# Weight units of a hybrid decoder layer placed at byte offsets 0, 32, 64 or 96 in their SBUF tiles

## The chip, the cores and the metric

The kernel runs on one core of one Trainium2 chip, in one launch. The metric is device time in microseconds (us) from the first to the last moment of the execution; lower is better. Each kernel is run several times and the median is compared. A profile of one execution shows what every engine of the core did: PE (TensorE: matmuls, with PEld for the loading of weights into the array), DVE (VectorE), ACT (ScalarE), POOL (GpSimd), SP (which issues most DMAs).

## The reference

One decoder layer on 512 tokens of width 1024, all in float32. Cut to what matters:

```python
h = rmsnorm(x)
q, k, v, xr, gr, g_attn, g_rnn = split(h @ w_in)        # w_in: 1024 x 7168
A = diff_attention(q, k, v)                              # 8 heads, causal, two softmaxes, shared bias
R = gelu(gr) * rg_lru(causal_conv4(xr))
x = x + (sigmoid(g_attn) * (A @ w_proj_attn) + sigmoid(g_rnn) * (R @ w_proj_rnn)) @ w_out
x = x + square(relu(rmsnorm(x) @ w_up)) @ w_down         # 1024 -> 4096 -> 1024
```

## The kernel before

Every large product runs as three matmuls of type float32r on TensorE (`mm3`, lines 125 to 127): each operand is split into a high part and the remainder, and hi*hi, hi*lo and lo*hi are added in PSUM. A matmul has a *stationary* operand of 128x128, which is loaded into the array beforehand by a weight load, and a *moving* operand of 256 or 512 columns, which is streamed through. The profile writes out<-in with the names of both. While one matmul streams its moving operand, the weight load of the next one reads its stationary operand, so two reads from SBUF run side by side nearly all the time.

Weights come in *units* of 128x1024 numbers (four k tiles of 256 columns). SP loads a raw unit (`wraw`, later `raw`), ACT rounds it into `whi`, DVE writes the remainder into `wlo`. There are four buffers of each kind in pool `wp`, and one more pair in pool `fin` for the MLP, which takes every fifth unit there (`own`). Class `Weights` keeps one queue of units each for attention (`wa`) and for the recurrent branch (`wb`); `cols` puts requests into it, `cast` splits a unit, `get` hands it out. The MLP has its own list of units (`ops`, `cast_hi`, `cast_lo`).

The stages, with the sides on which the weight units stand:

- gates: `cols_proj` with weights stationary and `hT` (the normed input, transposed) moving, 512 columns. The same form serves the recurrent projections, then the attention projection (`aT` moving), the recurrent projection (`R`), the output projection (`mT`), and the MLP's up projection (`h2T` moving).
- q, k, v: `tok_proj` has tokens of `hT` stationary and the weight units `whi`, `wlo` *moving*, 256 columns. Four head pairs j = 0 to 3, filled in between the steps of attention.
- MLP down (line 1093): seven products of a Strassen-like scheme, weights stationary, the squared activations `us` moving, 256 columns. The up projection fills `us` in four chunks d, and after each chunk two halves m of the down projection follow.

The order on each engine is the order in which the program is written (helper `InOrder`; most ACT, DVE and POOL rows therefore carry line 66). The placement of tiles in SBUF is that of the pools. As built, every `whi` and `wlo` buffer in `wp` starts at a byte address that leaves 64 when divided by 128 (25920, 30016, 34112, 38208 and 42304, 46400, 50496, 54592), and the pair in `fin` at one that leaves 0. `hT`, `mT` and one of three `us` buffers (units of chunks n with n % 3 = 0) leave 64, `h2T`, `R`, `hu` and the other two `us` buffers leave 0, and `aT` leaves 96. Offsets within these tiles are multiples of 512 bytes, so every operand keeps the remainder of its tile.

Of the kernel before, what the change touches and what calls it, by code (L numbers as in the profile page):

```python
# [12 lines left out]
F32R = mybir.dt.float32r  # L13
# [6 lines left out]
P = 128  # L20
# [3 lines left out]
KT = DM // P  # L24
# [13 lines left out]
def tile_block(ctx: ExitStack, tc: tile.TileContext, x, w_in, w_rga, w_rgx, w_pa, w_pr, w_o,  # L38
# [5 lines left out]
    wp = ctx.enter_context(tc.tile_pool(name="wp", bufs=3))  # L44
# [13 lines left out]
    class InOrder:  # L58
        def __init__(self, engine):
            self.engine = engine  # L60
# [15 lines left out]
    def psum(tag):  # L76
        return pp.tile([P, 512], F32, tag=tag, name=tag, bufs=nb[tag])

    slots = [4]

    class Weights:
        def __init__(self, ahead, raws):
            self.reqs, self.raw, self.units = [], [], []
            self.pos, self.done, self.ahead, self.raws = 0, 0, ahead, raws

        def cols(self, w, c0, k0=0, n=KT):
            for k0 in range(k0, k0 + n, 4):
                self.reqs.append((w[k0 // 4, c0 // 256], 4))
            return self

        def fetch(self):
# [3 lines left out]
                nc.sync.dma_start(raw, src.rearrange("p (k c) -> p k c", k=a))  # L95
                self.raw.append(raw)

        def cast(self, pool=None):
            assert pool or slots[0] > 0
            slots[0] -= 0 if pool else 1  # L100
            self.fetch()
            n = len(self.units)
            raw, a = self.raw[n], self.reqs[n][1]
            hi, lo = ((pool or wp).tile([P, a, 1024 // a], F32R, tag=t, name=t, bufs=2 if pool else 4) for t in ("whi", "wlo"))
            A.copy(hi, raw)
            V.tensor_tensor(out=lo, in0=raw, in1=hi.bitcast(F32), op=ALU.subtract)
            self.raw[n] = None
            self.units.append((hi, lo))
            self.fetch()
# [14 lines left out]
    def mm3(o, l, r, first, last):  # L124
        T.matmul(o, l[0], r[0], start=first, stop=False)  # L125
        T.matmul(o, l[0], r[1], start=False, stop=False)  # L126
        T.matmul(o, l[1], r[0], start=False, stop=last)  # L127

    def split(hi, lo, src, scale=None):
        if scale is None:  # L130
            A.copy(hi, src)
            V.tensor_tensor(out=lo, in0=src, in1=hi.bitcast(F32), op=ALU.subtract)
        else:
            A.activation(hi, src, AF.Copy, scale=scale)
            V.scalar_tensor_tensor(out=lo, in0=src, scalar=scale, in1=hi.bitcast(F32), op0=ALU.mult, op1=ALU.subtract)
# [67 lines left out]
    def rstd_of(dst, ss, n, width):  # L203
        t = sm.tile([P, width], F32, tag="ms", name="ms")
        V.tensor_scalar(out=t, in0=ss, scalar1=1.0 / n, scalar2=EPS, op0=ALU.mult, op1=ALU.add)
        G.tensor_tensor(out=dst, in0=t, in1=mhalf[:, :width], op=ALU.pow)
# [22 lines left out]
    OQ, OK_, OV, OX, OG, OGA, OGR = (j * DM for j in range(7))  # L229
    wa = Weights(2, 2)  # L230
    wa.cols(w_in, OGA + 512)
    for j in range(4):
        for o in (OQ, OK_, OV):
            wa.cols(w_in, o + 256 * j)
    wa.cols(w_in, OGA + 768)
    for j in range(4):
        wa.cols(w_in, OGR + 256 * j)
    for j in range(4):
        wa.cols(w_pa, 256 * j)
    wb = Weights(1, 1)  # L240
    for j in range(4):
        wb.cols(w_in, OX + 256 * j).cols(w_in, OG + 256 * j)
    for j in range(4):
        wb.cols(w_pr, 256 * j)
    for j in range(4):
        wb.cols(w_o, 256 * j)
    R, aT, mT = [None] * KT, [None] * NH, [None] * KT
    tgr, tga = [None] * KT, [None] * KT
    es_act = ExitStack()
# [15 lines left out]
    with tc.tile_pool(name="p1", bufs=1) as p1:  # L265
        on = p1.tile([P, P], F32, name="on")
        G.memset(on, 1.0)
        zero = p1.tile([P, 256], F32R, name="zero")
        V.memset(zero.bitcast(F32), 0.0)
        pw = psum("acc")  # L270
        for n in range(16):
            T.matmul(pw[:, :256], zero[:, :P], zero, start=True, stop=True)
        ssq = p1.tile([P, S], F32, name="ssq")
        xT = p1.tile([P, KT, S], F32, name="xT")
        hu = [p1.tile([P, KT, S], F32R, name=f"hu{z}", tag=f"hu{z}") for z in range(2)]
        raws = [[(wp if u else p1).tile([P, 4, 256], F32, name="wraw", tag="wraw", bufs=2) for u in range(2)] for z in range(2)]
        pieces = ((0, 1), (1, 2), (2, 4), (4, 6), (6, 8))
        for k0, k1 in pieces:
            nc.sync.dma_start(xT[:, k0:k1, :], x[k0 * P:k1 * P, :].rearrange("(k p) s -> p k s", p=P))
            if k0 == 0:  # L280
                nc.sync.dma_start(smt, smalls)
            for z in range(2):
                c0 = 256 * (k0 % 4)
                nc.sync.dma_start(raws[z][k0 // 4][:, k0 % 4:(k1 - 1) % 4 + 1, :],
                                  w_in[k0 // 4, OGA // 256 + z][:, c0:c0 + 256 * (k1 - k0)].rearrange("p (k c) -> p k c", c=256))
        wa.fetch()
        ws = [[[wp.tile([P, 4, 256], F32R, tag=t, name=t, bufs=4) for t in ("whi", "wlo")] for u in range(2)] for z in range(2)]
        ps = [[psum("at"), psum("at")] for z in range(2)]
        for k0, k1 in pieces:
            u, kk = k0 // 4, slice(k0 % 4, (k1 - 1) % 4 + 1)  # L290
            for k in range(k0, k1):
                split(hu[0][:, k, :], hu[1][:, k, :], xT[:, k, :], smt[:, C_G1 + k:C_G1 + k + 1])
                if k == k0:
                    for z in range(2):
                        split(ws[z][u][0][:, kk, :], ws[z][u][1][:, kk, :], raws[z][u][:, kk, :])
            for k in range(k0, k1):
                sq = ssq if k == 0 else p1.tile([P, S], F32, tag="sq", name="sq", bufs=2)
                A.activation(sq, xT[:, k, :], AF.Square)
                if k:
                    V.tensor_tensor(out=ssq, in0=ssq, in1=sq, op=ALU.add)  # L300

        def two(k):
            for z in range(2):
                for c in range(2):
                    w = ws[z][k // 4]
                    cs = slice(c * P, (c + 1) * P)
                    mm3(ps[z][c], (w[0][:, k % 4, cs], w[1][:, k % 4, cs]), (hu[0][:, k, :], hu[1][:, k, :]), k == 0, k == KT - 1)

        for k in range(6):
            two(k)  # L310
        slots[0] = 2
        wa.cast()
        pr = psum("at")
        for t in range(NT):
            T.matmul(pr[:, t:t + 1], ssq[:, t * P:(t + 1) * P], ones, start=True, stop=True)
        rs = sm.tile([P, NT], F32, tag="rs4", name="rs4")
        rstd_of(rs, pr[:, :NT], DM, NT)
        dg = p1.tile([P, S], F32, name="dg", tag="sq", bufs=2)
        for t in range(NT):
            A.activation(dg[:, t * P:(t + 1) * P], ident, AF.Copy, scale=rs[:, t:t + 1])  # L320
        two(6)
        wa.cast()
        rb = p1.tile([P, S], F32, name="rb")
        gu = cols_proj(wa, lambda k: (hu[0][:, k, :], hu[1][:, k, :]), lambda ps: gate_out(tga, 2, ps, rb))
        pb = psum("acc")
        T.matmul(pb, on, dg, start=True, stop=True)
        V.tensor_copy(rb, pb)
        two(7)
        slots[0] += 2
        for k in range(KT + 1):  # L330
            if k < KT:
                V.tensor_tensor(out=xT[:, k, :], in0=xT[:, k, :], in1=rb, op=ALU.mult)
            if k > 0:
                split(hT[0][:, k - 1, :], hT[1][:, k - 1, :], xT[:, k - 1, :], smt[:, C_G1 + k - 1:C_G1 + k])
                next(gu)
        wa.pump()
        for z in range(2):
            gate_out(tga, z, ps[z], rb)
# [482 lines left out]
    fin = ctx.enter_context(tc.tile_pool(name="fin", bufs=1, reuse_waits="tile"))  # L821
# [79 lines left out]
    added, cast = set(), set()  # L901
# [12 lines left out]
    def cast_hi():  # L914
        n = len(units)
        plus(n)
        slots[0] -= 1
        kind, a, p = ops[n]
        src = raw[kind, a, p if kind == "up" else uses[p][0]]
        own = n % 5 == 4  # L920
        hi, lo = ((fin if own else wp).tile([P, 4, 256], F32R, tag=t, name=t, bufs=1 if own else 4) for t in ("whi", "wlo"))
        A.copy(hi, src)
        units.append((hi, lo))
        half.append((hi, lo, src, ops[n]))
# [19 lines left out]
    def ahead():  # L944
        if half:
            cast_lo()
        if can_cast():
            cast_hi()
# [105 lines left out]
    for n, (kind, a, p, pairs) in enumerate(steps):  # L1054
        o = kind, a, p
# [11 lines left out]
        hi, lo = units[number[o]]  # L1067
# [19 lines left out]
        k = seen.get(o, 0)  # L1087
# [53 lines left out]
```

## Time and profile before

| | |
|---|---|
| time, median of 3 runs | 880.63 us (880.16 to 881.45) |
| the profiled execution | 880.92 us, its span 879.2 us |
| PE busy | 871.2 us, 5232 matmuls |
| PEld busy | 762.6 us |
| DVE / ACT / POOL busy | 602.2 / 429.0 / 64.4 us |
| DMA | 99.28 MB, mean 113 GB/s |

Times in the profile count from the start of the span. Busy time of PE is the union of its matmuls, which overlap: a matmul's duration in the table of groups is longer than the distance from its start to the next start. What PE costs is therefore read from that distance (here called the *cadence*), in a stretch of known matmuls.

### The profile page before, as it was taken

What the parts mean: (1) busy time and instruction counts of PE and PEld (TensorE: products, weight loads), DVE (VectorE), ACT (ScalarE), POOL (GpSimd) and SP (SyncE); (2) the same over time, 40 slices, a digit from 0 to 9 for tenths busy, and PEclk for the clock granted to TensorE, in tenths of its full rate; (3) what the DMA queues carried; (4) which work ended last, traced back from release to release, by engine and by line L of the source; (5) the groups of instructions that cost most, each with busy time, mean ns of one, the idle gap of its engine ahead of it and who ended that gap; (6) DMA issues with size and microseconds to landing.
All of it is one profiled execution on the core that took longest, in us unless ns stands there. A gap on an engine that the chain in (4) does not pass through costs nothing.

```text
span 879.2 us, 13193 instructions
## 1 busy us (share of the span) xinstructions
PE 871.2 (99%) x5232; PEld 762.6 (87%) x5232; DVE 602.2 (68%) x1040; ACT 429.0 (49%) x683; POOL 64.4 (7%) x72
## 2 busy tenths in 40 slices
PE   9999999999999999999999999999999999999997
PEld 7799999999888887888878888889988998899897
DVE  6765688887866346877876656767746775667586
ACT  7444355554555336577643235556335444544441
POOL 0030222113000000000000000000000000000000
PEclk9999999999999999999999999999999999999999
DMA  5347222131321342322213633223642364256353
GB/s 200 135 142 222 93 73 77 52 94 62 98 70 39 113 137 95 110 85 88 80 55 125 223 125 114 102 86 82 170 166 72 110 173 134 64 137 194 78 146 95
DMA packets 34238, 99.28 MB, mean 113 GB/s; under 512 B 3952, under 2 KB 8760, under 8 KB 34176
## 3 DMA queue, kind: packets, MB, share of 16 engines
q1 hardware_dynamic: 30976, 87.93, 30.3%
q0 software_dynamic: 3200, 10.50, 6.3%
q8 instruction: 41, 0.67, 0.3%
q14 instruction: 21, 0.17, 0.1%
HBM read 87.89 MB, written 4.76 MB: 105 GB/s over the span
## 4 chain that ended last, share of the span: by engine, by line
PE 88%; ACT 4%; DMA 3%; DVE 3%; issue 1%; SPq 0%; POOL 0%; ACTq 0%; DVEq 0%; POOLq 0%
PE acc L125 21%; PE acc L126 21%; PE acc L127 20%; PE acc L1093 17%; PE at L507 3%; DMA wraw<-in_w_in_dram 2%; ACT whi L66 1%; DVE wlo L66 1%; PE at L541 1%; PE at L126 1%; PE at L127 1%; PE at L125 1%; PE at L459 1%; PE at L572 1%; DMA xT<-in_x_dram 1%
## 5 line engine op out<-in xcount | busy, mean ns | idle before, releaser
L1093 PE MATMUL acc<-us,whi 128*128 128x256 f32 x896 | 158.9, 281 | 0.5 <-DVE x L66 0.5
L66 DVE TENSOR_TENSOR wlo<-wraw,whi 128x1024 fp32r<-128x1024 f32 (+2 forms) x86 | 96.9, 1148 | 67.9 <-ACT whi L66 67.6
L66 ACT CAST whi<-raw 128x1024 fp32r<-128x1024 f32 x88 | 90.5, 1048 | 104.2 <-DVE raw L66 39.4
L1093 PEld LDWEIGHTS acc<-us,whi 128*128 128x128 f32 x896 | 137.7, 189 | 1.2 <-DVE x L66 0.7
L1093 PE MATMUL acc<-us,wlo 128*128 128x256 f32 x448 | 125.4, 280 | 0.0
L66 DVE TENSOR_TENSOR wlo<-raw,whi 128x1024 fp32r<-128x1024 f32 x88 | 106.8, 1220 | 17.1 <-ACT whi L66 17.0
L125 PE MATMUL acc<-whi,hT 128*128 128x256 f32 x384 | 111.4, 290 | 0.0
L127 PE MATMUL acc<-whi,hT 128*128 128x256 f32 x384 | 108.9, 284 | 0.0
L126 PE MATMUL acc<-wlo,hT 128*128 128x256 f32 x384 | 108.9, 284 | 0.0
L66 ACT CAST whi<-wraw 128x1024 fp32r<-128x1024 f32 (+2 forms) x86 | 82.5, 982 | 50.0 <-DMA wraw<-in_w_in_dram 33.6
L126 PE MATMUL acc<-h2T,whi 128*128 128x512 f32 x256 | 100.5, 392 | 0.0
L125 PE MATMUL acc<-h2T,whi 128*128 128x512 f32 x256 | 100.1, 391 | 0.0
L127 PE MATMUL acc<-h2T,wlo 128*128 128x512 f32 x256 | 100.0, 390 | 0.0
L1093 PEld LDWEIGHTS acc<-us,wlo 128*128 128x128 f32 x448 | 84.2, 188 | 0.0
L125 PE MATMUL acc<-hT,whi 128*128 128x512 f32 x208 | 82.2, 395 | 0.0
L127 PE MATMUL acc<-hT,wlo 128*128 128x512 f32 x208 | 81.5, 392 | 0.0
L126 PE MATMUL acc<-hT,whi 128*128 128x512 f32 x208 | 81.5, 392 | 0.0
L125 PEld LDWEIGHTS acc<-whi,hT 128*128 128x128 f32 x384 | 73.2, 191 | 4.3 <-issue 3.0
L127 PEld LDWEIGHTS acc<-whi,hT 128*128 128x128 f32 x384 | 73.2, 191 | 0.8 <-issue 0.4
L126 PEld LDWEIGHTS acc<-wlo,hT 128*128 128x128 f32 x384 | 73.3, 191 | 0.7 <-issue 0.5
L66 ACT ACTIVATE pe<-pe,nm 128x128 f32<-128x128 f32 (+3 forms) x64 | 35.5, 556 | 65.4 <-DVE nm L66 65.4
L66 DVE TENSOR_TENSOR x<-acc,x 128x512 f32<-128x512 f32 x48 | 33.0, 688 | 40.9 <-PE acc L1093 31.5
(194 smaller groups left out, 1609.9 us busy)
## 6 DMA issues: line engine op xcount, KB each, us to landing
wraw<-in_w_in_dram SPq DMA_DIRECT2D x52, 512.0 KB, 3.5
raw<-in_w_up_dram SPq DMA_DIRECT2D x32, 512.0 KB, 4.4
raw<-in_w_dn_dram SPq DMA_DIRECT2D x32, 512.0 KB, 3.4
raw<-raw POOLq DMA_DIRECT2D x16, 512.0 KB, 4.5
wraw<-in_w_pa_dram SPq DMA_DIRECT2D x8, 512.0 KB, 4.3
wraw<-in_w_pr_dram SPq DMA_DIRECT2D x8, 512.0 KB, 3.4
wraw<-in_w_o_dram SPq DMA_DIRECT2D x8, 512.0 KB, 4.4
trep<-tdram SPq DMA_DIRECT2D x8, 320.0 KB, 4.9
```

Source lines behind the costliest of these rows:

```text
L66: ins = f(*a, **k)
L125: T.matmul(o, l[0], r[0], start=first, stop=False)
L126: T.matmul(o, l[0], r[1], start=False, stop=False)
L127: T.matmul(o, l[1], r[0], start=False, stop=last)
L459: T.transpose(out=ps[:, t * P:(t + 1) * P], in_=qn[t // 2][:, c0:c0 + P], identity=ident)
L507: T.matmul(lg[c][:, :N], qT[r, x0, i * P:(i + 1) * P], kT[r, y0, :N], start=a == 0, stop=a == 2)
L541: T.transpose(out=tp[:, b * P:(b + 1) * P], in_=st[s][:, b * P:(b + 1) * P], identity=ident)
L572: T.matmul(ps[:, t:t + 1], sq[:, t * P:(t + 1) * P], ones, start=True, stop=True)
L1093: T.matmul(b[:, 256 * u:256 * u + 256], l[:, i, P * u:P * u + P], act[:, r, f, i % 2], start=p in ("M1", "M2", "M5") and k == z == u == e ...
```

## The change

A helper `weight_pair` makes every pair of `whi` and `wlo`. The tiles get 32 more numbers (128 bytes) per partition, and the unit lies 8 * shift numbers, that is 32 * shift bytes, behind the tile's start. `shift` is 0 to 3: the head pair j for q, k and v, the output group j in the other projections (0 for the two gate groups OGA + 512 and OGA + 768 and for the first two groups), a // 2 % 4 for a unit of the MLP's up projection, and (2 * chunk + half) % 4 for the down projection. Two arguments that were never used (`k0`, `n` of `cols`, and `pool` of `cast`) go.

```diff
+    def weight_pair(a, shift, own=None):
+        ts = [(own or wp).tile([P, 1024 + 32], F32R, tag=t, name=t, bufs=1 if own else 4) for t in ("whi", "wlo")]
+        return [t[:, 8 * shift:8 * shift + 1024].rearrange("p (k c) -> p k c", k=a) for t in ts]
...
-            hi, lo = ((pool or wp).tile([P, a, 1024 // a], F32R, tag=t, name=t, bufs=2 if pool else 4) for t in ("whi", "wlo"))
+            hi, lo = weight_pair(a, self.shift[n])
...
     for j in range(4):
         for o in (OQ, OK_, OV):
-            wa.cols(w_in, o + 256 * j)
+            wa.cols(w_in, o + 256 * j, j)
     wa.cols(w_in, OGA + 768)
     for j in range(4):
-        wa.cols(w_in, OGR + 256 * j)
+        wa.cols(w_in, OGR + 256 * j, j)
...
-        ws = [[[wp.tile([P, 4, 256], F32R, tag=t, name=t, bufs=4) for t in ("whi", "wlo")] for u in range(2)] for z in range(2)]
+        ws = [[weight_pair(4, 0) for u in range(2)] for z in range(2)]
...
-        own = n % 5 == 4
-        hi, lo = ((fin if own else wp).tile([P, 4, 256], F32R, tag=t, name=t, bufs=1 if own else 4) for t in ("whi", "wlo"))
+        shift = a // 2 % 4 if kind == "up" else (2 * a[0] + a[1]) % 4
+        hi, lo = weight_pair(4, shift, fin if n % 5 == 4 else None)
```

The same edit as for OGR is made for `w_pa`, OX, OG, `w_pr` and `w_o`. Each engine has the same instructions in the same order with the same waits as before; what differs is the SBUF address of operands. Since the tiles grow by 128 bytes, all other tiles keep their remainder by 128. The weight units of shift 0, 1, 2, 3 now start at addresses that leave 64, 96, 0 and 32 (in the `fin` pair 0, 32, 64 and 96).

More of the change, by code (lines that the diff above doesn't have):

```diff
@@ L79, in tile_block, with cols @@
     slots = [4]
+    def weight_pair(a, shift, own=None):
+        ts = [(own or wp).tile([P, 1024 + 32], F32R, tag=t, name=t, bufs=1 if own else 4) for t in ("whi", "wlo")]
+        return [t[:, 8 * shift:8 * shift + 1024].rearrange("p (k c) -> p k c", k=a) for t in ts]
     class Weights:
         def __init__(self, ahead, raws):
-            self.reqs, self.raw, self.units = [], [], []
+            self.reqs, self.raw, self.units, self.shift = [], [], [], []
             self.pos, self.done, self.ahead, self.raws = 0, 0, ahead, raws
-        def cols(self, w, c0, k0=0, n=KT):
-            for k0 in range(k0, k0 + n, 4):
+        def cols(self, w, c0, shift=0):
+            for k0 in range(0, KT, 4):
                 self.reqs.append((w[k0 // 4, c0 // 256], 4))
+                self.shift.append(shift)
             return self
@@ L96, in fetch, with cast @@
                 self.raw.append(raw)
-        def cast(self, pool=None):
-            assert pool or slots[0] > 0
-            slots[0] -= 0 if pool else 1
+        def cast(self):
+            assert slots[0] > 0
+            slots[0] -= 1
             self.fetch()
@@ L233, in tile_block @@
         for o in (OQ, OK_, OV):
-            wa.cols(w_in, o + 256 * j)
+            wa.cols(w_in, o + 256 * j, j)
     wa.cols(w_in, OGA + 768)
     for j in range(4):
-        wa.cols(w_in, OGR + 256 * j)
+        wa.cols(w_in, OGR + 256 * j, j)
     for j in range(4):
-        wa.cols(w_pa, 256 * j)
+        wa.cols(w_pa, 256 * j, j)
     wb = Weights(1, 1)
     for j in range(4):
-        wb.cols(w_in, OX + 256 * j).cols(w_in, OG + 256 * j)
+        wb.cols(w_in, OX + 256 * j, j).cols(w_in, OG + 256 * j, j)
     for j in range(4):
-        wb.cols(w_pr, 256 * j)
+        wb.cols(w_pr, 256 * j, j)
     for j in range(4):
-        wb.cols(w_o, 256 * j)
+        wb.cols(w_o, 256 * j, j)
     R, aT, mT = [None] * KT, [None] * NH, [None] * KT
```

## The prediction

> **What bounds the kernel.** I read the page first: the summary, the clock row and the chain that ended last.
>
> ```profile
> span 879.2 us, 13193 instructions
> PE 871.2 (99%) x5232; PEld 762.6 (87%) x5232; DVE 602.2 (68%) x1040; ACT 429.0 (49%) x683; POOL 64.4 (7%) x72
> ...
> PEclk9999999999999999999999999999999999999999
> ...
> PE 88%; ACT 4%; DMA 3%; DVE 3%; issue 1%; SPq 0%; POOL 0%; ACTq 0%; DVEq 0%; POOLq 0%
> ```
>
> PE is busy for 871.2 of 879.2 us at an undisturbed clock, and 88% of the chain is PE. The windows say where the other 8 us lie.
>
> ```profile
> core 0: us, PE busy (x) PEld busy (x) DVE busy (x) ACT busy (x) POOL busy (x), PEclk, DMA share, GB/s
> 0.00:800.00 800.00, 797.11 (x4700) 693.06 (x4701) 550.12 (x976) 401.42 (x650) 60.95 (x68) 1.00 0.36 111
> 800.00:879.00 79.00, 74.04 (x535) 69.53 (x533) 52.03 (x64) 27.60 (x33) 3.44 (x4) 1.00 0.47 134
> ```
>
> Up to 800 us PE rests for 2.9 us in all (800.00 less 797.11); the other 5.0 us stand in the last stretch. A nanosecond more per matmul is thus a nanosecond more of the span, with no slack to take it up. The change adds no matmul, so the question is what each costs. The groups name the forms:
>
> ```profile
> L1093 PE MATMUL acc<-us,whi 128*128 128x256 f32 x896 | 158.9, 281 | 0.5 <-DVE x L66 0.5
> ...
> L1093 PE MATMUL acc<-us,wlo 128*128 128x256 f32 x448 | 125.4, 280 | 0.0
> L125 PE MATMUL acc<-whi,hT 128*128 128x256 f32 x384 | 111.4, 290 | 0.0
> ...
> L126 PE MATMUL acc<-h2T,whi 128*128 128x512 f32 x256 | 100.5, 392 | 0.0
> ...
> L126 PE MATMUL acc<-hT,whi 128*128 128x512 f32 x208 | 81.5, 392 | 0.0
> ...
> L126 PE MATMUL acc<-aT,whi 128*128 128x512 f32 x64 | 25.4, 397 | 0.0
> ```
>
> The third number of a row is the mean duration (281 ns for 256 columns, 392 for 512), but matmuls overlap, so the price is the cadence. I took windows in which one form runs without a break, each beginning 0.06 us after a start. Each count holds two matmuls that run at the left edge already; the window divided by the count less two is the cadence.
>
> ```profile
> core 0: us, PE busy (x) PEld busy (x) DVE busy (x) ACT busy (x) POOL busy (x), PEclk, DMA share, GB/s
> 45.13:56.51 11.38, 11.38 (x97) 11.38 (x96) 8.06 (x17) 7.64 (x11) 2.17 (x6) 1.00 0.34 106
> 808.63:811.51 2.88, 2.88 (x26) 2.88 (x26) 1.82 (x2) 1.06 (x1) 0.00 (x0) 1.00 0.59 191
> 772.76:781.12 8.36, 8.36 (x73) 8.36 (x72) 5.36 (x10) 6.52 (x10) 0.00 (x0) 1.00 0.38 98
> 797.75:808.63 10.88, 10.88 (x98) 10.88 (x98) 7.39 (x8) 4.21 (x4) 0.00 (x0) 1.00 0.93 273
> 292.22:311.03 18.81, 18.81 (x85) 15.52 (x84) 5.34 (x5) 5.88 (x8) 2.17 (x3) 1.00 0.39 112
> 495.08:538.65 43.57, 43.57 (x194) 36.05 (x193) 25.35 (x34) 16.50 (x22) 0.00 (x0) 1.00 0.45 156
> 761.60:767.04 5.44, 5.44 (x26) 4.50 (x25) 3.22 (x7) 4.80 (x8) 0.00 (x0) 1.00 0.10 19
> 458.67:495.08 36.41, 36.41 (x161) 29.87 (x160) 22.84 (x28) 11.66 (x14) 0.00 (x0) 1.00 0.44 143
> 739.63:761.60 21.97, 21.97 (x98) 18.03 (x97) 14.27 (x20) 12.17 (x19) 0.86 (x1) 1.00 0.26 68
> 446.31:450.98 4.67, 4.67 (x22) 3.76 (x21) 4.57 (x8) 1.71 (x3) 0.00 (x0) 1.00 0.25 99
> ```
>
> In these rows PE is busy throughout and the clock is 1.00, yet equal shapes have different prices. I set against them the addresses that the built program gives: the *relation* of a matmul is the address of its moving operand less that of the weights that are loaded while it streams, modulo 128 bytes.
>
> - 256 columns, relation 0: 11.38 / 95 = 119.8 ns (row 1: q, k, v, both at 64) and 2.88 / 24 = 120.0 (row 2: down, both at 0).
> - 256, relation 64: 8.36 / 71 = 117.7 and 10.88 / 96 = 113.3 (rows 3 and 4: down, `us` at 0, weights at 64). Row 2 follows row 4 directly: only the weights go over to the `fin` pair, and each matmul costs 6.7 ns more.
> - 512, relation 0: 18.81 / 83 = 226.6, 43.57 / 192 = 226.9, 5.44 / 24 = 226.7 (rows 5 to 7: `hT`, `mT`, `h2T` with the `fin` pair).
> - 512, relation 64: 36.41 / 159 = 229.0, 21.97 / 96 = 228.9 (rows 8 and 9: `R`, `h2T`).
> - 512, relation 32: 4.67 / 20 = 233.5 (row 10: `aT`, at 96, with weights at 64).
>
> So the two reads disturb each other, by an amount that hangs on their relation, and by 120.0 in both the (64, 64) and the (0, 0) rows it is the relation and not the address that counts, at least in steps of 64. This is what the change touches. PEld shows how tight it is: with 256 columns the weight loads are busy throughout (11.38 of 11.38), with 512 for some 83% (36.05 of 43.57).
>
> **The change part by part.**
>
> *Casts.* ACT and DVE write the units at other offsets. Outputs at 96 and at 0 can be compared (the first two rows are casts of weight units):
>
> ```profile
> L66 DVE TENSOR_TENSOR wlo<-raw,whi 128x1024 fp32r<-128x1024 f32 x88 | 106.8, 1220 | 17.1 <-ACT whi L66 17.0
> ...
> L66 ACT CAST whi<-raw 128x1024 fp32r<-128x1024 f32 x88 | 90.5, 1048 | 104.2 <-DVE raw L66 39.4 <-DMA raw<-raw 20.0 <-PE acc L1093 17.8
> ...
> L66 DVE SCALAR_TENSOR_TENSOR aT<-of,sg,aT 128x512 fp32r<-128x512 f32 x8 | 6.0, 752 | 6.4 <-ACT aT L66 6.4
> L66 DVE SCALAR_TENSOR_TENSOR h2T<-x,smt,h2T 128x512 fp32r<-128x512 f32 x8 | 6.0, 752 | 6.3 <-ACT h2T L66 6.3
> ...
> L66 ACT ACTIVATE h2T<-x,smt 128x512 fp32r<-128x512 f32 x8 | 5.8, 724 | 25.1 <-DVE x L66 20.5 <-DMA raw<-in_w_up_dram 4.6
> ...
> L66 ACT ACTIVATE aT<-of,sg 128x512 fp32r<-128x512 f32 x8 | 5.8, 723 | 11.8 <-DVE of L66 11.8
> ```
>
> 752 and 752 ns on DVE, 723 and 724 on ACT for `aT` and `h2T`: I cost this at nothing. What hides a change there is that PE waits for ACT or DVE hardly at all; were the casts longer, a wait of PE for a unit would come next.
>
> *Raw loads, waits, order:* unchanged; nothing.
>
> *Matmuls.* From the addresses in both built programs, the matmuls with a weight unit on one side, by relation 0 / 32 / 64 / 96:
>
> - 256 columns: 1689 / 0 / 802 / 4 before, 571 / 661 / 673 / 590 after.
> - 512 columns: 926 / 188 / 994 / 4 before, 477 / 449 / 683 / 503 after.
>
> So a quarter of the matmuls of each kind goes to each relation, and the relations 32 and 96, which were 196 of 4607, become 2203.
>
> *512 columns.* Relations 0, 64 and 32 are priced by rows: 226.8, 228.95, 233.5 ns. 449 fewer at 226.8 (-101.8 us), 311 fewer at 228.95 (-71.2), 261 more at 233.5 (+60.9), 499 more at relation 96, which no row shows. Its bounds are the lowest and the highest row, 226.8 and 233.5: +113.2 or +116.5 us, sum +1.1 or +4.4. Relation 96 is as far from a multiple of 64 as 32 is, but its moving operand is aligned where that of `aT` is not; I take the middle, 230.15 (+114.8): **+2.7 us**.
>
> *256 columns.* 1118 fewer at 119.9 (-134.05), 129 fewer at 115.5 (the middle of 113.3 and 117.7; -14.9), and 1247 more at relations 32 and 96, which no row of this width shows. From below: they behave like relation 64, 115.5, +144.0, sum -4.9 (at 113.3 even -7.7). From above: they carry the whole extra of 512 columns, 233.5 - 226.8 = 6.7, on top of 119.9, 126.6 ns: +157.9, sum +8.9. I take 119.9, since the weight loads have no slack at this width, and the nearest rows with a full weight path are those of 120: +149.5, **+0.6 us**.
>
> Sum +3.3 us on the profiled execution's 880.92, 884.2. That execution lies 0.29 us above the median of 880.63, so the median becomes **883.9 us**, 0.4% slower.
>
> The Trainium skill speaks against any effect: "SBUF — State Buffer", section "Who interferes with whom", gives PE one read port for the moving operand and another, independent one for weight loads, and says that PE never waits on anyone. By it the sum would be 0. Rows 2 and 4 disagree, 120.0 against 113.3 ns for the same instruction.
>
> Another page, "TensorE: Matmul & The Clock Gate", has a spacing of N / 2.4 GHz + 2.5 ns; by it an estimate for 256 and 512 columns is 109.2 and 215.8 ns, below every row here. No run here shows matmuls at that spacing, so the room between it and the rows is no gain that I count.
>
> **The rivals.**
>
> 1. *Both widths pay in full.* If 32 and 96 each cost what row 10 shows, the sum is +4.4 + 8.9 = +13.3: 893.9 us. For it: row 10 is the only one with an offset of 32, and it is the dearest. Against it: the moving side alone may be what costs there, and in the 512-column products the units are never the moving side.
> 2. *An offset of 32 acts like the multiple of 64 below it.* Then only `aT`, whose moving side is off by 32 before and after, keeps its 233.5. With 512 columns relations 0 and 64 stay near halves, sum 0. With 256 the new 1247 cost the mean of 119.9 and 115.5, 117.7: +146.8 - 148.95 = -2.2 us, 878.5. For it: rows tell 0 from 64 clearly. Against it: row 10, unless the moving side alone explains it, and then pairs 1 and 3 of q, k, v, 576 matmuls, pay up to 6.7 ns (+3.9) and the sum is above zero.
> 3. *The staggered reads avoid each other with 256 columns* (the other side). q, k and v run at relation 0 throughout, a bad one; anything else may be like 113.3 to 117.7. With 512 at its low end: -4.9 + 1.1 = -3.8, 876.8 us. The place is the 576 matmuls of pairs 1 and 3 and the 672 of the second halves of down. It decides from a cadence at 32 and 96 below (148.95 - 1.1 - 1.8) / 1247 = 117.1 ns, where the gain passes 0.2%.
> 4. *No sum.* The prices come from the stages and not from the addresses, or gains and losses cancel: 880.6. Against the first: rows 2 and 4, 6 and 8 adjoin in time and differ. "SBUF — State Buffer" of the Trainium skill, in the section named above, would have this outcome.
>
> **How the numbers follow.** What a measurement of this kernel can tell from no change is about 0.2%, 1.8 us. My forecast (32-byte relations cost with 512 columns, little with 256) has 0.46, with its own range 881.5 to 887; some 0.06 of that lies within 0.2%. Rival 1 has 0.15 (all slower), between half its price and the whole. Rival 2 has 0.17, 0.10 of it faster and 0.07 within; rival 3 has 0.10, faster; rival 4 has 0.12, within. That gives 0.20 faster, 0.25 same, 0.55 slower. The range must leave out no more than 2 in 10: it goes down to 877.5, which leaves out most of rival 3, and up to 890, which takes in the lower half of rival 1.
>
> **What would show it.** In the changed profile: the attention projection's second output group (`aT` at 96, weights at 96, relation 0) should fall from 233.5 to about 226.8 ns, its first stay; pair 2 of q, k, v should fall from 119.8 to 113 to 118; the output projection, 226.9 throughout before, should step by output group to 226.9, (unknown), 229 and 233.5. The second halves of each down chunk and pairs 1 and 3 show the price at relations 32 and 96; there the forecast breaks if they stand below 117 or above 123 ns. It also breaks if groups with the same relation but another address differ, or if casts become longer than the 1220 and 1048 ns of the rows above, with PE waiting for them.

## The result, and the profile after

The changed kernel takes 885.55 us (median of 5 runs, 884.60 to 886.16) against 881.35 us for the kernel before (5 runs beside it, 880.16 to 881.45). The ratio is 1.0051 [1.0036, 1.0065]: 0.5% slower. The profiled execution took 885.55 us, with a span of 883.8 us against 879.2. These are lines of the page of the changed kernel: span, busy engines, granted clock, shares of the chain that ended last.

```profile
span 883.8 us, 13193 instructions
PE 875.8 (99%) x5232; PEld 761.1 (86%) x5232; DVE 601.9 (68%) x1040; ACT 428.7 (49%) x683; POOL 64.5 (7%) x72
...
PEclk9999999999999999999999999999999999999999
...
PE 88%; ACT 4%; DMA 4%; DVE 3%; issue 1%; SPq 0%; POOL 0%; ACTq 0%; DVEq 0%; POOLq 0%
```

PE is busy 4.6 us longer, and the span is 4.6 us longer; the other engines and the clock are as they were. The windows of the changed kernel over the same two stretches as before show whether PE waits somewhere (columns: busy time and instructions of each engine, clock, DMA share, GB/s).

```profile
core 0: us, PE busy (x) PEld busy (x) DVE busy (x) ACT busy (x) POOL busy (x), PEclk, DMA share, GB/s
0.00:800.00 800.00, 797.13 (x4666) 687.32 (x4667) 546.95 (x974) 401.08 (x650) 60.48 (x68) 1.00 0.35 110
800.00:879.00 79.00, 78.56 (x568) 73.76 (x567) 53.60 (x66) 27.62 (x34) 4.01 (x5) 1.00 0.48 135
```

Up to 800 us PE rests for 2.87 us, against 2.89 before: no wait was added. In the same 800 us it began 34 matmuls fewer (4666 against 4700). So matmuls became dearer. Nor did the casts change, by the groups of the changed kernel:

```profile
L66 DVE TENSOR_TENSOR wlo<-raw,whi 128x1024 fp32r<-128x1024 f32 x88 | 106.6, 1217 | 17.4 <-ACT whi L66 17.3
...
L66 ACT CAST whi<-raw 128x1024 fp32r<-128x1024 f32 x88 | 90.5, 1048 | 105.1 <-DVE raw L66 39.7 <-DMA raw<-raw 20.3 <-PE acc L1098 17.2
```

1217 and 1048 ns, before 1220 and 1048. The sums of start-to-start distances by stage tell where the time went. With 512 columns: gates and recurrent projections (`hT`) 144.5 to 147.3 us, up (`h2T`) 175.8 to 178.3, output projection 43.6 to 44.5, `R` 45.0 to 45.6, `aT` 44.9 to 44.6, `hu` 35.5 to 35.3; together 489.3 to 495.6, +6.3 us. With 256 columns: q, k, v 142.4 to 140.8, down 159.3 to 159.1, together -1.8 us. The net is +4.5 us.

The clearest place is the output projection, whose moving operand `mT` stays at one address while the units change. Before, it ran at 226.9 ns from end to end. Its eight units of the changed kernel, in order of time (windows chosen as in the prediction, so 5.34 us with a count of 25 is 23 distances):

```profile
core 0: us, PE busy (x) PEld busy (x) DVE busy (x) ACT busy (x) POOL busy (x), PEclk, DMA share, GB/s
496.36:501.70 5.34, 5.34 (x25) 4.33 (x24) 3.84 (x9) 2.20 (x3) 0.00 (x0) 1.00 0.77 265
501.70:507.15 5.45, 5.45 (x26) 4.50 (x25) 2.70 (x4) 1.05 (x1) 0.00 (x0) 1.00 0.90 333
507.15:512.75 5.60, 5.60 (x26) 4.51 (x25) 2.79 (x5) 3.43 (x5) 0.00 (x0) 1.00 0.46 185
512.75:518.35 5.60, 5.60 (x26) 4.50 (x25) 2.99 (x4) 1.05 (x1) 0.00 (x0) 1.00 0.57 178
518.35:523.85 5.50, 5.50 (x26) 4.50 (x25) 2.69 (x5) 3.42 (x5) 0.00 (x0) 1.00 0.03 10
523.85:529.45 5.60, 5.60 (x26) 4.49 (x25) 2.62 (x4) 0.00 (x0) 0.00 (x0) 1.00 0.24 94
529.45:535.06 5.61, 5.61 (x26) 4.52 (x25) 3.92 (x7) 3.79 (x6) 0.00 (x0) 1.00 0.00 0
535.06:540.66 5.60, 5.60 (x26) 4.50 (x25) 3.58 (x4) 1.54 (x2) 0.00 (x0) 1.00 0.59 200
```

That is 232.2, 227.1, 233.3, 233.3, 229.2, 233.3, 233.8 and 233.3 ns. By the relation modulo 128 rows 1 and 2 are the same (0), and so are 5 and 6 (64), yet one of each pair is 4 to 5 ns dearer. Modulo 256 the eight rows stand at 128, 0, 224, 96, 64, 192, 160 and 32, and only 0 and 64 are cheap. The difference comes from the padding: a tile of 1056 numbers is 4224 bytes, 33 times 128. The four `whi` buffers, all at 64 modulo 256 before, now lie at 64, 192, 64, 192. So every second buffer has another relation even where the change leaves the offset at 0.

Over all matmuls, the mean cadence by relation modulo 256 in the changed kernel is, at 0 / 32 / 64 / 96 / 128 / 160 / 192 / 224: with 512 columns 228.8, 233.1, 229.7, 233.4, 232.7, 234.0, 233.1, 233.0 ns; with 256 columns 118.8, 117.3, 116.5, 119.6, 119.0, 118.0, 116.7, 118.5 ns. A period of 512 does not show: with 512 columns relation 0 modulo 512 costs 229.1 ns and 256 costs 228.6, 64 costs 229.9 and 320 costs 229.6.

### The profile page after: what moved, and what is told of

It reads as the page before. It is cut to its first block, busy times and chain, and to the rows that moved or that the text cites. A ratio compares the mean times of both kernels' runs of the same rounds, so it can differ in the third digit from the quotient of the medians.

```text
span 883.8 us, 13193 instructions
## 1 busy us (share of the span) xinstructions
PE 875.8 (99%) x5232; PEld 761.1 (86%) x5232; DVE 601.9 (68%) x1040; ACT 428.7 (49%) x683; POOL 64.5 (7%) x72
## 4 chain that ended last, share of the span: by engine, by line
PE 88%; ACT 4%; DMA 4%; DVE 3%; issue 1%; SPq 0%; POOL 0%; ACTq 0%; DVEq 0%; POOLq 0%
PE acc L130 21%; PE acc L132 21%; PE acc L131 21%; PE acc L1098 17%; PE at L512 3%; DMA wraw<-in_w_in_dram 2%; ACT whi L66 1%; DVE wlo L66 1%; PE at L546 1%; PE at L131 1%; PE at L132 1%; PE at L130 1%; PE at L464 1%; PE at L577 1%; DMA xT<-in_x_dram 1%
## 5 line engine op out<-in xcount | busy, mean ns | idle before, releaser
L66 ACT CAST whi<-raw 128x1024 fp32r<-128x1024 f32 x88 | 90.5, 1048 | 105.1 <-DVE raw L66 39.7
L66 DVE TENSOR_TENSOR wlo<-raw,whi 128x1024 fp32r<-128x1024 f32 x88 | 106.6, 1217 | 17.4 <-ACT whi L66 17.3
L66 ACT ACTIVATE pe<-pe,nm 128x128 f32<-128x128 f32 (+3 forms) x64 | 35.5, 556 | 65.5 <-DVE nm L66 63.4
```

Of the source, the lines that this page charges most:

```text
L66: ins = f(*a, **k)
```

## The experiments

Two theories stood against each other. A: the price hangs on the difference of the two addresses modulo 256, and with 512 columns 128 and 192 cost some 5 and 4 ns more than 0 and 64. B: the relation modulo 128 is all there is, and the aligned matmuls became dearer for another reason (their neighbours, or this one execution). Each microsecond figure below is the measured ratio times the kernel before. Where a tile pair is "one tile", `whi` and `wlo` are halves of a tile of 2112 numbers, 8448 bytes (33 times 256), so that all buffers keep one remainder modulo 256.

**The padding alone** (the changed kernel with no offset):

```diff
-        return [t[:, 8 * shift:8 * shift + 1024].rearrange("p (k c) -> p k c", k=a) for t in ts]
+        o = 0
+        return [t[:, o:o + 1024].rearrange("p (k c) -> p k c", k=a) for t in ts]
```

> The longer tiles (1056 numbers) with every unit at the start of its tile. Theory A (the cadence hangs on the difference of the two addresses modulo 256 bytes; the longer tile alone puts every second buffer 128 bytes off): the 512-column matmuls of relations 0 and 64 go half to 128 and 192, 228 to 232.6 and 229.6 to 233.2 ns, +3.7 us; 256 columns -0.2 us; in all +3.4 us against before (some 884.6), and about two thirds of the changed kernel's loss without any shift. Theory B (modulo 128; what rose in the aligned matmuls of the changed kernel came from their shifted neighbours or from the execution): no difference to before, 0 +- 0.8 us, and 512-column relations 0 and 64 at 227 to 229 ns in every buffer.

Measured: 884.78 us, ratio 1.0038 [1.0025, 1.0052], +3.3 us. Two windows of its output projection, units at relation 0 and then at 128:

```profile
502.34:513.23 10.89, 10.89 (x50) 9.01 (x49) 5.33 (x8) 4.48 (x6) 0.00 (x0) 1.00 0.70 263
513.23:524.38 11.15, 11.15 (x50) 9.04 (x49) 5.91 (x8) 4.49 (x6) 0.00 (x0) 1.00 0.29 94
```

10.89 / 48 = 226.9 and 11.15 / 48 = 232.3 ns. The padding by an odd multiple of 128 bytes costs most of what the whole change costs, with every unit still at offset 0.

**The offsets alone** (one tile, offset as in the change):

```diff
+        t = (own or wp).tile([P, 2048 + 64], F32R, tag="whl", name="whl", bufs=1 if own else 4)
+        o = 8 * shift
+        return [t[:, o + z:o + z + 1024].rearrange("p (k c) -> p k c", k=a) for z in (0, 1024)]
```

> The shifts of the changed kernel, but high and low part in one tile whose length is a multiple of 256 bytes, so that the buffers stay alike. Theory A: 512 columns +4.5 us, 256 columns -1.0 us, in all +3.5 us against before. Theory B: +2.4 us, and the aligned relations (modulo 128) back at 228 to 229 ns. Both: relations 32 and 96 at 233 to 234 ns with 512 columns.

Measured: 885.49 us, 1.0041 [1.0028, 1.0053], +3.6 us. Its output projection, relation 0 and then 192:

```profile
495.61:506.28 10.67, 10.67 (x49) 8.82 (x48) 6.54 (x11) 3.25 (x4) 0.00 (x0) 1.00 0.83 295
...
517.48:528.67 11.19, 11.19 (x50) 9.02 (x49) 5.30 (x8) 3.43 (x5) 0.00 (x0) 1.00 0.15 55
```

10.67 / 47 = 227.0 and 11.19 / 48 = 233.1 ns. The padding (+0.38%) and the offsets (+0.41%) don't add up to the whole (+0.51%). That fits the table above: a unit that its offset has already put at about 233 ns stays there when its buffer lies at 128.

**All units moved by 128 bytes** (one tile, `o = 32` throughout). By A every 512-column matmul leaves 0 and 64; by B nothing changes.

> Every unit 128 bytes behind the start of its tile, tiles a multiple of 256 bytes, no shift by 32. Modulo 128 bytes every relation is that of before; modulo 256 all of 0 become 128 and all of 64 become 192. Theory A: 512 columns from 228 and 229.5 to 232.6 and 233.2 ns, +7.6 us, 256 columns -0.5 us; in all +7.2 us, some 888. Theory B: 0 +- 0.8 us.

Measured: 885.10 us, 1.0044 [1.0032, 1.0057], +3.9 us. Output projection at 128, up at 192, a stretch of down at 192:

```profile
497.26:541.86 44.60, 44.60 (x194) 36.17 (x193) 25.40 (x34) 16.48 (x22) 0.00 (x0) 1.00 0.45 160
570.06:592.46 22.40, 22.40 (x98) 18.05 (x97) 15.37 (x24) 12.24 (x18) 0.00 (x0) 1.00 0.29 94
788.74:799.65 10.91, 10.91 (x98) 10.91 (x98) 9.67 (x11) 4.00 (x4) 0.86 (x1) 1.00 0.57 146
```

44.60 / 192 = 232.3 (before 226.9), 22.40 / 96 = 233.3 (before 228.9), 10.91 / 96 = 113.6 ns. B is out: a move of 128 bytes changes prices. A had the sum too high (+7.2 us). The 256-column stages gained more than it priced (q, k, v 142.4 to 141.2 us, down 159.3 to 157.9), and the `hT` products lost 2.2 us, not the 2.8 that A's price gives.

**One tile without offset**, the control for the new tile: `o = 0`.

> Control for e2 to e6: high and low part in one tile, no offset, every relation as in before. Both theories: 0 +- 0.8 us against before. If it is not 0, the one tile (the cast of the high part then waits for the last reader of both halves) has a price of its own, which has to be taken from e2 to e6.

Measured: 881.35 us, 1.0002 [0.9993, 1.0011]. So the tile itself has no price that shows.

**The moving side moved instead** (from the kernel before; units untouched). This tells the difference of the addresses from the units' own address. The tiles behind `hT` in memory (`hu`, `R`, `h2T`, `us`) move with it; `mT` doesn't.

```diff
-    hT = hp.tile([P, 2, KT, S], F32R, tag="hT", name="hT")
+    hT = hp.tile([P, 2 * KT * S + 32], F32R, tag="hT", name="hT")[:, 32:].rearrange("p (z k s) -> p z k s", z=2, k=KT)
```

> The weight units stay as in before; hT alone (not mT, not us) moves by 128 bytes, and with it hu, R, h2T and the two us buffers behind it, since the tile is 128 bytes longer. If it is the difference of the two addresses that counts: hT and h2T products 128 and 192 instead of 0 and 64, 232.4 and 233.2 ns, hT +2.8, h2T +2.3, R +0.7, hu +0.5 us; mT unchanged at 226.9; in all +6.0 us by the changed kernel's prices (some 887). If it is the address of the weight units that counts (where they start, or that they lie off a 256-byte step): 0.

Measured: 885.53 us, 1.0049 [1.0036, 1.0062], +4.3 us. Windows of `hT`, `mT`, `h2T`:

```profile
291.48:310.76 19.28, 19.28 (x85) 15.64 (x84) 5.66 (x6) 6.64 (x9) 2.17 (x3) 1.00 0.37 110
496.32:539.88 43.56, 43.56 (x194) 36.03 (x193) 25.32 (x34) 16.50 (x22) 0.00 (x0) 1.00 0.45 158
567.98:590.38 22.40, 22.40 (x98) 18.05 (x97) 15.48 (x24) 12.25 (x18) 0.00 (x0) 1.00 0.28 94
```

19.28 / 83 = 232.3 (before 226.6), 43.56 / 192 = 226.9 (unmoved, unchanged), 22.40 / 96 = 233.3 ns (before 228.9). With the units where they always were, the products whose moving operand moved lost the same 4 to 6 ns. It is the difference that counts. The sum again fell short of the price (+6.0 us): `hT` lost 1.9 us and not 2.8, `hu` lost nothing, and q, k, v (-1.2 us) and down (159.3 to 158.9) gained.

**Offsets by the rule.** One tile; each stage names the remainder modulo 256 at which its units shall lie, so that all 512-column products come to relation 0 and the 256-column ones to 64. The last number of `cols` and the `shift` of down are that remainder: 64 for `hT` and `mT`, 128 for `hu`, `R`, `h2T` and q, k, v, 224 for `aT`, 64 for down (with one of the three `us` buffers moved by 64 bytes).

```diff
+        o = (shift - (128 if own else 64)) % 256 // 4
...
+            wa.cols(w_in, o + 256 * j, 128)
...
+        wa.cols(w_pa, 256 * j, 224)
...
+        shift = 128 if kind == "up" else 64
```

> Offsets chosen by the changed kernel's prices: weights at relation 0 modulo 256 in every 512-column product (attention, recurrent, up and output projections, gates), at relation 64 in q, k, v and in down (with the one us buffer moved by 64 bytes for that). Theory A: 512 columns -2.4 us (the attention projection from 233.9 to about 228), 256 columns -4.5 us (q, k, v from 119.7 to about 117, down's relation 0 to about 115), in all -6.9 us against before, some 874. Theory B: -6.7 us, the same. A rival for both: that the cadence in a stage is set by something else in the stage: then 0.

Measured: 877.76 us, 0.9953 [0.9940, 0.9965], -4.1 us. Windows of `R`, of up, and of a down chunk:

```profile
456.44:492.29 35.85, 35.85 (x160) 29.65 (x159) 22.61 (x28) 11.66 (x14) 0.00 (x0) 1.00 0.44 140
554.69:601.90 47.21, 47.21 (x210) 39.04 (x209) 35.76 (x49) 24.93 (x37) 1.77 (x2) 1.00 0.25 74
602.13:641.58 39.45, 39.45 (x337) 39.45 (x336) 29.46 (x35) 17.87 (x21) 1.71 (x2) 1.00 0.60 169
```

`R` fell to 35.85 / 158 = 226.9 (from 229.0), up to 47.21 / 208 = 227.0 (from 228.9), as priced; `aT` only to 230.5. `R` has both operands at remainder 128 here and costs what `mT` costs with both at 64 in the kernel before. The sum was priced at -6.9 us; what failed is down: 39.45 / 335 = 117.8 ns throughout this chunk, though the kernel before has 113.3 at the same relation in the fourth window that the prediction shows.

**Down at 192** (`shift = 128 if kind == "up" else 192`): does the relation settle which of the two prices comes, or can both come at either relation?

> As e4_best, but the down weights at relation 192 instead of 64. In e4_best all of down ran at 117.8 ns, where the kernel before had runs of 113.3 at the same relation; in e3_all_plus128 relation 192 ran at 113.3 wherever the unit before it had 192 too. If 192 settles at 113.3 by itself: 1340 matmuls x 4.4 ns = -5.9 us against e4_best, -9.5 us against before (some 872). If the two cadences are two states of either relation, and which one comes is set by a disturbance ahead: 117.5 to 117.8 ns again, 877.5.

Measured: 877.38 us, 0.9957 [0.9945, 0.9970], no change. A down chunk:

```profile
604.37:643.83 39.46, 39.46 (x337) 39.46 (x336) 29.39 (x35) 17.87 (x21) 1.71 (x2) 1.00 0.60 170
```

117.8 ns again, and 113.3 only in the last chunk. So one relation has two prices.

**q, k, v at 192 too** (`wa.cols(w_in, o + 256 * j, 0)`):

> As e5, and q, k, v at relation 192 instead of 64 too (weights 64 bytes before hT modulo 256 instead of behind). By the changed kernel's prices q, k, v stay at 117.5 ns and the time equals e5 within 0.5 us. If 192 settles at 113.3 in this stage: 1070 x 4 ns, -4.3 us against e5.

Measured: 874.93 us, 0.9938 [0.9924, 0.9951], 2.5 us below the last one; between the two expectations. The mean of q, k, v fell from 117.7 to 115.2 ns. Its first long stretch:

```profile
44.72:55.51 10.79, 10.79 (x97) 10.79 (x96) 7.50 (x15) 7.65 (x11) 2.18 (x6) 1.00 0.35 108
```

10.79 / 95 = 113.6 ns; other stretches of the stage ran at 117.8, and three of the four down chunks stayed there.

**Every fifth unit of down at another relation.** In the kernel before, the third down chunk ran at 117.7 ns until a unit of relation 0, and at 113.3 after it. If such a unit ends the dear price, placing one in every five should pay for itself. The edit starts from the last version.

```diff
-        shift = 128 if kind == "up" else 192
+        shift = 128 if kind == "up" else 128 if n % 5 == 4 else 64
```

> As e6_tok192_down192 (875 us), with down at relation 64 and its every fifth unit (the fin pair) at relation 0. In the kernel before, down's third chunk had just this mix: 117.8 ns until the first unit of relation 0, 113.3 in all units of relation 64 after it. If a unit of another relation resets the lock: 1054 matmuls from 117.6 to about 113.5 (-4.3 us), 289 from 117.6 to 120 (+0.7), -3.6 us against e6, some 871. If the state comes from something else: 117.8 stays and the fifth units cost +0.7 us.

Measured: 872.52 us (4 runs), 0.9897 [0.9880, 0.9913]. The first down chunk, in order of time: at 64, the first unit at 0, at 64 again:

```profile
600.29:605.94 5.65, 5.65 (x50) 5.65 (x49) 2.65 (x7) 4.06 (x8) 0.00 (x0) 1.00 0.64 158
605.94:608.81 2.87, 2.87 (x26) 2.87 (x26) 2.87 (x4) 2.45 (x3) 0.00 (x0) 1.00 0.11 20
608.69:619.58 10.89, 10.89 (x98) 10.89 (x98) 10.02 (x11) 2.83 (x3) 0.85 (x1) 1.00 0.68 190
```

5.65 / 48 = 117.7, 2.87 / 24 = 119.6, 10.89 / 96 = 113.4 ns: here the 117.7 ends with the dearer unit. Over the stage, relation 64 has a mean of 114.7 ns and relation 0 of 119.5. It is no fixed rule. Of the eleven stretches of 24 matmuls or more that follow such a unit directly, ten ran at the low price; the last one, in the last chunk, did not (first the end of a unit at 0, then 64):

```profile
854.90:857.42 2.52, 2.52 (x23) 2.52 (x23) 0.77 (x2) 1.05 (x1) 0.00 (x0) 1.00 0.28 52
857.54:865.90 8.36, 8.36 (x73) 8.36 (x72) 5.08 (x7) 0.00 (x0) 0.00 (x0) 1.00 0.22 73
```

2.52 / 21 = 120.0 and 8.36 / 71 = 117.7 ns. Nor does it take such a unit. In the version "Offsets by the rule" all of down is at 64, yet in its last chunk these two stretches stand one behind the other:

```profile
842.28:847.49 5.21, 5.21 (x48) 5.21 (x47) 4.41 (x5) 1.05 (x1) 0.86 (x1) 1.00 0.63 204
847.86:856.34 8.48, 8.48 (x74) 8.48 (x74) 8.38 (x11) 4.01 (x4) 0.48 (x1) 1.00 0.62 157
```

5.21 / 46 = 113.3 and 8.48 / 72 = 117.8 ns. All that lies between them are two longer distances, of 149 and 224 ns.

**The same at 192, with the fifth unit at 128** (`128 if kind == "up" else 0 if n % 5 == 4 else 192`):

> The same with down at relation 192 and every fifth unit at 128, the mix of the third chunk of e3_all_plus128 (113.3 to 114.1 and 118.2 ns). If a unit of another relation resets the lock: -3.3 us against e6, some 871.5. If not: 117.8 stays, +0.2 us.

Measured: 871.50 us (4 runs), 0.9893 [0.9878, 0.9908]: the fastest version, 1.1% below the kernel before and 1.6% below the change. Its first unit at 128, and the stretch after it:

```profile
605.30:608.15 2.85, 2.85 (x26) 2.85 (x26) 2.85 (x4) 2.57 (x3) 0.00 (x0) 1.00 0.07 17
608.15:619.05 10.90, 10.90 (x98) 10.90 (x98) 10.02 (x11) 2.83 (x3) 0.85 (x1) 1.00 0.67 189
```

118.8 and 113.5 ns: the same change. Here all eleven stretches of 24 or more behind such a unit settled at the low price.

## Why the prediction was right, and which steps were off

The direction held, and so did the kind of mechanism: the two reads disturb each other by an amount that hangs on the difference of their addresses. That the size came close (+3.3 us forecast, +4.6 on the profiled executions) is in part luck. The period of that difference was wrong; the terms for 512 and 256 columns missed by +3.6 and -2.4 us, in opposite directions; and the padding, which had no term of its own, costs +3.3 us alone.

- *Casts and waits at nothing:* held (1217 and 1048 ns; PE's rest 2.87 us).
- *The difference counts, not the address:* held; shown from the moving side by the run with `hT` moved. "SBUF — State Buffer" of the Trainium skill, section "Who interferes with whom", by which PE's two read ports are independent and PE never waits on anyone, disagrees with the 232.3 ns of that run against 226.6 in the kernel before, where nothing but addresses was changed; the measurement decides.
- *Modulo 128 bytes:* wrong. This is the step that failed: the prediction took "relation 0 / 32 / 64 / 96" for the whole of it. It had no row that could tell 128 from 0, since all buffers lay alike modulo 256 before, and it looked at the offsets while the length of the padded tile moved every second buffer. The runs show 232.3 at 128 and 233.3 at 192, where it priced 226.8 and 228.95. One of its own signs of breaking came true here: groups with the same relation but another address differ.
- *512 columns, +2.7 us:* measured +6.3. By the mean cadence over all matmuls in both traces, relation 0 (modulo 128) rose from 228.17 to 230.91 ns, 477 x 2.74 = 1.3 us; relation 64 from 229.12 to 231.61, 683 x 2.49 = 1.7 us. Both are mostly the modulus: at 0 and 64 modulo 256 the changed kernel has 228.8 and 229.7. Relation 96, unseen before and taken as 230.15, came out at 233.15, like 32 (233.56): 503 x 3.0 = 1.5 us. The middle of the two bounds was the wrong choice; the dearer bound, the row of `aT`, was right. Those three come to 4.5 us. Against them stands -0.6 us, since the 449 matmuls that left relation 0 had cost 228.17 and not 226.8; the -0.3 that is left of the difference of 3.6 was not traced. The price of 32 was right by luck: modulo 256 the row of `aT` stands at 160, and that 32 costs the same (233.1) no row showed.
- *256 columns, +0.6 us:* measured -1.8. Relations 32 and 96, taken as 119.9, came out at 117.71 and 118.99 ns, -1.4 and -0.5 us; relation 0 fell by 0.8 ns on 571 matmuls, -0.4 us. The full load path did not make them dear. This is rival 3 in part, with a mean of 118.3 ns where it needed 117.1 to decide; it took back some of what the 512 columns cost.
- *Rivals 1 and 2:* the extra of 512 columns never showed with 256 (rival 1), and an offset of 32 does not act like the multiple of 64 below it: 233.3 against 227.1 ns with `mT` (rival 2).
- *What would show it:* `aT`'s second group should have fallen to 226.8; it fell to 230.9 at relation 0 and 232.4 at 128, while the first stayed at about 233.5. Pair 2 of q, k, v fell to 117.5, within 113 to 118. With 256 columns relations 32 and 96 stood at 117.7 and 119.0 ns in the mean, between 117 and 123. The output projection did step, but within each group too, by buffer.

Open: whether the disturbed read is the load of the next weights or something tied to the matmul's own weights (within a unit the two have one remainder, and there are too few borders between units to tell); why the period is 256 bytes; why `hT` and `aT`, whose products are interleaved with other matmuls, stay at 229.1 and 230.5 ns at relation 0; why one `hT` stretch of the changed kernel at relation 64 ran at 232.9; and what sets which of its two prices a 256-column stretch at 64 or 192 gets.

## What to carry to other kernels

Where PE never waits and its weight loads run beside the matmuls, compare the cadence of equal shapes across the kernel, and set it against the difference between the two operands' addresses: neighbouring stretches of one form with another tile are an experiment that the profile has already made. Before an offset or a pad is costed, work out where every rotating buffer comes to lie; a tile length that is an odd multiple of 128 bytes changes every second one. Here the best difference was 0 modulo 256 bytes with 512 columns, and 64 or 192 with 256 columns, with a unit of another relation now and then; the last part is a finding of two versions, not a rule.

## What the runs showed of the hardware

- Back-to-back matmuls of 512 columns cost 226.6 to 227.1 ns at an address difference of 0 modulo 256 bytes, about 229 at 64, and 232 to 234 at 32, 96, 128, 160, 192 and 224. Where products are interleaved with other matmuls, relation 0 has 229.1 (`hT`) and 230.5 ns (`aT`).
- With 256 columns at 64 or 192 there are two lasting prices, 113.3 to 113.6 and 117.7 to 117.8 ns, for up to 115 and 335 matmuls on end. In seven kernels all 202 unbroken stretches of 14 matmuls or more at such a relation settled at one of them, 86 at the cheap one and 116 at the dear one. Behind a unit of another relation, itself at 118.8 to 120.0 ns, the cheap one came in 21 of 22 stretches of the two versions that placed such units; behind a longer distance between two matmuls either came. What decides was not found.
- ACT and DVE wrote the units at any of the offsets in the same mean time (1048 ns; 1217 against 1220 ns).
